# A hybrid decoder layer: attention merges moved from ScalarE and GpSimd to VectorE, branch sums to VectorE, x rows loaded ahead of merged blocks

## The chip, the cores and the metric

The kernel runs on one NeuronCore of a Trainium2 chip. The time is the device time of one execution in microseconds; the median of several runs is compared. TensorE (PE, with its weight loads PEld), VectorE (DVE), ScalarE (ACT) and GpSimd (POOL) each work through a queue of their own in order. SyncE (SP) issues nearly all DMA transfers, also in order: an issue that waits holds back those behind it. PSUM holds the matmuls' results; a tile of it is free again once another engine has read it.

## What is computed

One decoder layer over 2048 tokens with 1024 channels, in float32:

```
h = rms_norm(x); proj = h @ w_in                      # 1024 x 9224
A: gated DeltaNet   q,k,v = silu(conv(proj)); chunk inverse; scan over time with states S
                    y_dn  = (rms_norm(o_dn) * silu(z)) @ w_branch_dn
B: dilated window attention, three groups (window, dilation), each with output o_g and log denominator
                    alpha = softmax over the groups' log denominators
                    o_swa = sum_g alpha_g * o_g
                    y_swa = (o_swa * silu(z)) @ w_branch_swa
merged = sigmoid(g_dn) * y_dn + sigmoid(g_swa) * y_swa
x      = x + merged @ w_out
```

The change touches three places: the sum over groups in `o_swa` (called a merge here), the sum of the two gated branches in `merged`, and the loads of the rows of `x` that the last line adds.

## The kernel before, in words

Each float32 operand is split into a high and a low part, so that a product is three matmuls. The program has these stages.

- Up to about 970 us: normalisation and the attention columns of `w_in`, with the attention itself beside them. For each of 16 tiles of 128 tokens it leaves in DRAM (`oscr`) the three groups' unnormalised outputs, four heads of 128 channels, each with two more columns: the negated score maximum and the sum of exponentials.
- Up to about 2003 us: 24 column blocks of 128 (z columns, DeltaNet columns, then 16 gate blocks), `cunits`, L710. A block is four units of 512 tokens, 24 matmuls of 128x512 each (L723 to L725). A gate unit's result stands in one of three PSUM buffers `mm` until ScalarE has taken its tanh (`g_block`, L1159) into one of two `gt` buffers, which SyncE stores to `gscr` (L1160). Beside these units run first the DeltaNet blocks' own work, then the chunk inverse on VectorE, the scan (16 steps over time, L1031 to L1146), and the merges.
- Branch products, about 2003 to 2207 us (`fin_y`): 8 blocks `nb` of 256 tokens, 8 pieces `m` of 128 output channels, each piece 24 matmuls of 128x256 (L1345 to L1347). L1349 gates both branches in PSUM on VectorE, L1351 adds them, L1352 stores the sum to `mscr`. `o_plan` and `o_prep` beside it load, transpose (L1314) and gate (L1315, with z from L1307) the next block's inputs. `g_load` (L1333) loads the gates three pieces ahead. Four times `wo_chunk` prepares a quarter of `w_out`.
- Output projection from 2207 us (`group`): 8 groups of 256 tokens, seven products of 12 matmuls of 128x512 each (L1424) in a Strassen-like scheme. `m_load` (L1359) loads the merged blocks, `m_op` splits them (L90, L91) and forms their sums (L1380); x rows (`xo`, L1398) are added to the products on GpSimd (L1408) and VectorE (L1411).

What orders the work: a counter `tick` goes up at every `hook()`, which stands after every six matmuls of a column unit and every twelve of a branch piece, and `self.at(d, f)` emits `f` at d ticks from now. In the branch products this is the order of all queues. In the column blocks from the inverse on, and in the output projection, a scheduler may still reorder what was so emitted.

A merge (`combine(t)`, L1255) before: VectorE takes the minimum of the negated maxima (L1252), GpSimd the differences (L1263), ScalarE their exponential (L1266), GpSimd the shares (L1267 to L1271; the reciprocal is a power of -1). ScalarE scales the 12 outputs of 128x128 (L1275), GpSimd adds the groups in two instructions of 128x512 (L1279), SyncE stores the result to `osd` (L1281). The input tile `oc` has two buffers: the load of merge t+2 (L1247) waits for the store of merge t. Merges are numbered 0 to 15 here. 6 to 15 run after the scan, beside the gate units.

In the scan, L1065 and L1072 prepare the block that a step multiplies with; L1084 and L1086 are products with the states, L1088 makes `rr` from them on VectorE, L1091 `qs` on ScalarE, L1095 multiplies `rr`, L1097 takes `vn`, L1101 and L1106 use it, L1103 updates the states on VectorE, L1122 scales the result, L1124 stores it.

Of the kernel before, what the change touches and what calls it, by code (L numbers as in the profile page):

```python
# [6 lines left out]
F32 = mybir.dt.float32  # L7
F32R = mybir.dt.float32r
AF = mybir.ActivationFunctionType
ALU = mybir.AluOpType  # L10
PSUM = bass.MemoryType.PSUM

P = 128
# [4 lines left out]
H = 4  # L18
# [25 lines left out]
def dr(ap, off, dims):  # L44
    return bass.AP(tensor=ap.tensor, offset=ap.offset + off, ap=[list(d) for d in dims])


class Net:
# [1184 lines left out]

    def comb_setup(self, M):
        self.M, self.ocs = M, {}
        self.mone = self.cb.tile([P, 4], F32, name="mone", bufs=1)
        self.nc.gpsimd.memset(self.mone, -1.0)
        self.comb_load(0)
        self.comb_load(1)
        self.at(6, lambda: self.comb_min(0))  # L1240
        self.at(11, lambda: self.combine(0))

    def comb_load(self, t):
        oc = self.ocs[t] = self.cb.tile([P, G, H, 130], F32, name="oc", bufs=2)
# [2 lines left out]
        self.nc.sync.dma_start(oc.rearrange("p g h c -> p (g h c)"),  # L1247
                               dr(self.oscr, t * P * G * H * 130, [[G * H * 130, P], [1, G * H * 130]]))

    def comb_min(self, t):  # L1250
        self.cs = self.cb.tile([P, 4, 12], F32, name="cs", bufs=2)
        self.nc.vector.tensor_reduce(out=self.cs[:, 0, 0:4].unsqueeze(2), in_=self.ocs[t][:, :, :, 128].rearrange("p g h -> p h g"),  # L1252
                                     axis=mybir.AxisListType.X, op=ALU.min)

    def combine(self, t):  # L1255
        nc, cb, V = self.nc, self.cb, self.nc.gpsimd
        oc, sm = self.ocs.pop(t), self.cs
        if 0 < t < 15:
            self.comb_load(t + 1)
        nm, ls = oc[:, :, :, 128], oc[:, :, :, 129]  # L1260
        mn, e, c, r = sm[:, 0, 0:4], sm[:, 1, :].rearrange("p (g h) -> p g h", h=H), \
            sm[:, 2, :].rearrange("p (g h) -> p g h", h=H), sm[:, 3, 0:4]
        V.tensor_tensor(out=e, in0=mn.unsqueeze(1).to_broadcast([P, G, H]), in1=nm, op=ALU.subtract)  # L1263

        def share():
            nc.scalar.activation(e, e, AF.Exp)  # L1266
            V.tensor_tensor(out=c, in0=e, in1=ls, op=ALU.mult)  # L1267
            V.tensor_tensor(out=r, in0=c[:, 0], in1=c[:, 1], op=ALU.add)
            V.tensor_tensor(out=r, in0=r, in1=c[:, 2], op=ALU.add)
            V.tensor_tensor(out=r, in0=r, in1=self.mone, op=ALU.pow)  # L1270
            V.tensor_tensor(out=c, in0=e, in1=r.unsqueeze(1).to_broadcast([P, G, H]), op=ALU.mult)  # L1271

        def weigh(g):
            for h in range(H):
                nc.scalar.activation(oc[:, g, h, 0:P], oc[:, g, h, 0:P], AF.Identity, scale=c[:, g, h:h + 1])  # L1275

        def add(g):
            o = oc[:, 0, :, 0:P]
            V.tensor_tensor(out=o, in0=o, in1=oc[:, g, :, 0:P], op=ALU.add)  # L1279
            if g == 2:  # L1280
                nc.sync.dma_start(dr(self.osd, t * P * 512, [[512, P], [P, H], [1, P]]), o)  # L1281
        self.at(2, share)
        for g in range(G):
            self.at(5 + g, lambda g=g: weigh(g))
        for g in (1, 2):
            self.at(6 + g, lambda g=g: add(g))
        if t < 15:
            self.at(9, lambda: self.comb_min(t + 1))
            self.at(15, lambda: self.combine(t + 1))

    def o_load(self, t):
        nc, fp = self.nc, self.fp
# [28 lines left out]
    def o_plan(self, nb, d):  # L1321
        self.z = getattr(self, "z", {})
        for j, (t, b) in enumerate(((2 * nb, 0), (2 * nb, 1), (2 * nb + 1, 0), (2 * nb + 1, 1))):
            self.at(max(1, d + 3 * j - 8), lambda t=t, b=b: self.z_load(t, b))
            self.at(d + 3 * j, lambda t=t, b=b: self.o_prep(t, b))
            if b and nb < 7:
                self.at(d + 3 * j + 1, lambda t=t: self.o_load(t + 2))
# [7 lines left out]
    def fin_y(self, nb, m):  # L1335
        nc = self.nc
        self.g_load(8 * nb + m + 3)
        gt = self.gt.pop(8 * nb + m)
        pr = self.ps.tile([P, 512], F32, name="mm", bufs=3)
        for b in range(2):  # L1340
            o = pr[:, b * 256:(b + 1) * 256]
            oh, ol = self.o_tiles(nb, b)
            for k in range(4):
# [4 lines left out]
            self.hook()  # L1348
        nc.vector.scalar_tensor_tensor(out=gt, in0=gt, scalar=1.0, in1=pr.rearrange("p (b c) -> p b c", c=256),  # L1349
                                       op0=ALU.add, op1=ALU.mult)  # L1350
        nc.gpsimd.tensor_tensor(out=gt[:, 0, :], in0=gt[:, 0, :], in1=gt[:, 1, :], op=ALU.add)  # L1351
        self.at(2, lambda: nc.sync.dma_start(dr(self.mscr, nb * P * 2048 + m * 256, [[2048, P], [1, 256]]), gt[:, 0, :]))  # L1352

    def m_load(self, g):
        if g < 8:
# [36 lines left out]
    def group(self, g):  # L1392
        nc, V, p2 = self.nc, self.nc.vector, self.p2
        acc, hold, xo = {}, {}, {}

        def x_load(t, c):
            xo[t, c] = p2.tile([P, 512], F32, name="xo", bufs=4)
            nc.sync.dma_start(xo[t, c], dr(self.i["x"], (2 * g + t) * P * D + c * 512, [[D, P], [1, 512]]))  # L1398
# [13 lines left out]
            nc.sync.dma_start(dr(self.out, (2 * g + t) * P * D + c * 512, [[D, P], [1, 512]]), add)  # L1412
        for t, c in ((0, 0), (0, 1), (1, 1), (1, 0)):
            x_load(t, c)
        for i, (_, tgt, first, wn) in enumerate(PROD):
            q = 7 * g + i
            self.at(1, lambda q=q: self.m_op(q + 4))
# [30 lines left out]
    def run(self):  # L1448
# [55 lines left out]
        sm = pool(cst, "sm")  # L1504
# [78 lines left out]
            self.flush()  # L1583
        fst.close()
        self.p2 = pool(p2st, "p2", "right")
        self.m_load(1)
        for g in range(8):
            self.group(g)
        self.flush()
# [43 lines left out]
```

## Time and profile before

| what | value |
|---|---|
| median of 3 runs | 2374.9 us (2374.2 to 2382.52) |
| the profiled execution | 2375.45 us, of it 2373.6 us span |
| granted TensorE clock, mean | 0.989 |
| busy: TensorE, VectorE, ScalarE, GpSimd | 2282.9, 1353.3, 979.7, 1004.8 us |
| TensorE idle, 1660 to 1866 us (scan) | 13.8 us |
| 1866 to 2003 us (gate units, merges 6 to 15) | 15.0 us |
| 2003 to 2207.5 us (branch products) | 7.3 us |
| 2207.5 to 2244 us (first output group) | 5.8 us |
| from 2244 us | 3.8 us |

Rows of the profile name an engine, a line of the kernel, the operation, and what it writes and reads. In a row of a timeline the start and the duration in us stand first; in a grouped row the count, the total in us and the mean in ns follow. A bracket with an arrow tells how long the engine had stood idle before the instruction and what ended that wait. SPq is SyncE's queue of DMA issues. A mean granted clock below 1 says that for part of the time TensorE ran slower.

### The profile page before, as it was taken

Reading aid. Unit: us, or ns where it says so; the run is one execution under the profiler, and the core shown is the slowest. Engines: PE = TensorE matmul, PEld = TensorE weight load, DVE = VectorE, ACT = ScalarE, POOL = GpSimd, SP = SyncE. Lnnn points to the kernel's source line nnn. Section 1 sums busy time; section 2 is a strip of 40 time slices with the busy share of each in tenths; the row PEclk is TensorE's granted clock in tenths of the full one; section 3 lists DMA queues with packets and bytes.
Section 4 is the critical chain, followed back from the end, with each engine's and each line's share of the span. In section 5 each row is a group of like instructions: output and inputs, shape, how many; then the busy total and the mean of one; then the engine's idle time right before and its main releaser. Section 6 shows DMA issues by size and latency. Waiting matters only on the chain. (4 is left out here: it accounts for less than half of the span.)

```text
span 2373.6 us, 43873 instructions
## 1 busy us (share of the span) xinstructions
PE 2282.9 (96%) x15120; PEld 2069.9 (87%) x15120; DVE 1353.3 (57%) x2788; ACT 979.7 (41%) x3151; POOL 1004.8 (42%) x1460
## 2 busy tenths in 40 slices
PE   7999999989999999999999999999999989999999
PEld 7999999889999999787788788888788767999787
DVE  6566586693545545536777759998244202544553
ACT  5345466642434435445666641111444454211221
POOL 6374275574303203304667441121433453554543
PEclk9999999999999999999999999999999999999999
DMA  9989989858887888744544452224677765788742
GB/s 304 322 280 312 286 276 281 263 168 260 254 262 241 257 262 274 240 122 105 147 115 114 119 143 65 78 71 147 191 200 207 220 205 173 229 263 239 245 153 92
DMA packets 557270, 485.82 MB, mean 205 GB/s; under 512 B 68280, under 2 KB 517112, under 8 KB 554104
## 3 DMA queue, kind: packets, MB, share of 16 engines
q1 hardware_dynamic: 556760, 482.95, 66.4%
q8 instruction: 120, 1.97, 0.3%
q14 instruction: 102, 0.84, 0.1%
q10 hardware_dynamic: 288, 0.07, 0.0%
HBM read 280.23 MB, written 202.67 MB: 203 GB/s over the span
## 5 line engine op out<-in xcount | busy, mean ns | idle before, releaser
L723 PE MATMUL mm<-hh,w 128*128 128x512 f32 x1152 | 464.8, 403 | 13.7 <-ACT gt L1159 13.7
L725 PE MATMUL mm<-hh,w 128*128 128x512 f32 x1152 | 458.9, 398 | 0.0
L724 PE MATMUL mm<-hl,w 128*128 128x512 f32 x1152 | 458.0, 398 | 0.0
L436 PE MATMUL mm<-w,hh 128*128 128x256 f32 x1760 | 326.8, 285 | 0.0
L723 PEld LDWEIGHTS mm<-hh,w 128*128 128x128 f32 x1152 | 220.7, 192 | 62.0 <-ACT gt L1159 16.7
L436 PEld LDWEIGHTS mm<-w,hh 128*128 128x128 f32 x1760 | 269.9, 189 | 0.0
L725 PEld LDWEIGHTS mm<-hh,w 128*128 128x128 f32 x1152 | 217.7, 189 | 47.3
L436 PE MATMUL mm<-hh 128*128 128x256 f32 x880 | 256.4, 291 | 0.0
L724 PEld LDWEIGHTS mm<-hl,w 128*128 128x128 f32 x1152 | 218.3, 190 | 42.5
L91 POOL TENSOR_TENSOR w<-raw,w 128x512 fp32r<-128x512 f32 x68 | 99.2, 1461 | 361.8 <-ACT w L90 361.6
L436 PE MATMUL mm<-hl,hh 128*128 128x256 f32 x880 | 248.8, 283 | 0.9 <-POOL hl L298 0.9
L436 PE MATMUL mm<-hh,hl 128*128 128x256 f32 x880 | 248.7, 283 | 0.0
L436 PE MATMUL mm<-w,hl 128*128 128x256 f32 x880 | 247.6, 281 | 0.0
L610 DVE CUSTOM_DVE_ANT_0 p<-sc,mask 128x128 f32<-128x128 f32 (+1 forms) x192 | 70.0, 365 | 214.9 <-PE sc L607 83.3
L371 POOL TENSOR_SCALAR st<-st 128x4 f32<-128x4 f32 x96 | 20.5, 213 | 370.1 <-ACT junk L370 368.1
L436 PEld LDWEIGHTS mm<-hl,hh 128*128 128x128 f32 x880 | 168.2, 191 | 1.3 <-POOL hl L298 1.3
L436 PEld LDWEIGHTS mm<-hh 128*128 128x128 f32 x880 | 168.2, 191 | 0.0
L436 PEld LDWEIGHTS mm<-hh,hl 128*128 128x128 f32 x880 | 168.0, 191 | 0.0
L436 PEld LDWEIGHTS mm<-w,hl 128*128 128x128 f32 x880 | 165.3, 188 | 0.0
L837 DVE SCALAR_TENSOR_TENSOR acc<-xr,cw,acc 128x512 f32<-128x512 f32 x144 | 121.2, 841 | 16.7 <-ACT acc L835 11.5
L594 ACT ACTIVATE kq<-tp 128x256 fp32r<-128x256 f32 x148 | 56.5, 382 | 178.6 <-PE tp L587 177.6
L370 ACT ACTIVATE junk<-rec 128x128 f32<-128x128 f32 x288 | 89.4, 310 | 54.9 <-DVE rec L364 47.3
(353 smaller groups left out, 5815.2 us busy)
## 6 DMA issues: line engine op xcount, KB each, us to landing
wdr<-w SPq DMA_DIRECT2D x56, 512.0 KB, 4.5
w<-wdr SPq DMA_DIRECT2D x54, 512.0 KB, 5.0
qk<-qks SPq DMA_DIRECT2D x212, 128.0 KB, 3.9
qks<-rec SPq DMA_DIRECT2D x96, 256.0 KB, 3.0
raw<-in_w_in_dram SPq DMA_DIRECT2D x68, 256.0 KB, 3.3
gscr<-gt SPq DMA_DIRECT2D x64, 256.0 KB, 2.8
gt<-gscr SPq DMA_DIRECT2D x64, 256.0 KB, 5.3
wdr<-hh SPq DMA_DIRECT2D x28, 512.0 KB, 4.8
```

The lines of the kernel that those rows point to most:

```text
L91: eng.tensor_tensor(out=l, in0=raw, in1=h.bitcast(F32), op=ALU.subtract)
L370: nc.scalar.activation(self.junk, src[:, j * P:(j + 1) * P], AF.Square, accum_out=st[:, j:j + 1])
L371: nc.gpsimd.tensor_scalar(out=st[:, 0:4], in0=st[:, 0:4], scalar1=1.0 / P, scalar2=EPS, op0=ALU.mult, op1=ALU.add)
L436: mm = lambda x, y, **kw: nc.tensor.matmul(o, x, y, skip_group_check=True, **kw)
L594: nc.scalar.activation(h, src, AF.Copy)
L610: nc.vector.tensor_tensor_reduce(out=p[:, lo:hi], in0=sc[:, lo:hi], in1=self.mask[:, slot * P + lo:slot * P + hi], scalar=3e38, scale=-SCA ...
L723: nc.tensor.matmul(pr, wh[:, k, :], a, start=(k == 0), stop=False)
L724: nc.tensor.matmul(pr, wh[:, k, :], b, start=False, stop=False)
L725: nc.tensor.matmul(pr, wl[:, k, :], a, start=False, stop=(k == KT - 1))
L837: nc.vector.scalar_tensor_tensor(out=acc, in0=xr[:, j:j + 512], scalar=w[:, j:j + 1], in1=acc, op0=ALU.mult, op1=ALU.add)
```

## The change

A merge is made by VectorE, but for the exponential on ScalarE and the two group sums, which stay on GpSimd: minimum, differences, products, sum, reciprocal, shares, and three weighings of 128x512 (one per group, the shares broadcast along the channels) in place of ScalarE's 12. `combine` starts at tick 8 and then every 13 ticks (before 11 and 15) and takes the minimum itself; the exponential is emitted with it. The two gated branches are added by VectorE; their store is emitted one tick after the piece (before two). `z_load` is emitted 6 ticks before its use (before 8), though never before the block's first tick. The load of merged block 1 comes after the first group's four loads of x rows.

```diff
 def comb_setup(self, M):
     self.M, self.ocs = M, {}
-    self.mone = self.cb.tile([P, 4], F32, name="mone", bufs=1)
-    self.nc.gpsimd.memset(self.mone, -1.0)
     self.comb_load(0)
     self.comb_load(1)
-    self.at(6, lambda: self.comb_min(0))
-    self.at(11, lambda: self.combine(0))
+    self.at(8, lambda: self.combine(0))
...
-def comb_min(self, t):
-    self.cs = self.cb.tile([P, 4, 12], F32, name="cs", bufs=2)
-    self.nc.vector.tensor_reduce(out=self.cs[:, 0, 0:4].unsqueeze(2), in_=self.ocs[t][:, :, :, 128].rearrange("p g h -> p h g"),
-                                 axis=mybir.AxisListType.X, op=ALU.min)
...
 def combine(self, t):
-    nc, cb, V = self.nc, self.cb, self.nc.gpsimd
-    oc, sm = self.ocs.pop(t), self.cs
+    nc, cb, V = self.nc, self.cb, self.nc.vector
+    oc = self.ocs.pop(t)
     if 0 < t < 15:
         self.comb_load(t + 1)
+    sm = cb.tile([P, 4, 12], F32, name="cs", bufs=2)
...
+    V.tensor_reduce(out=mn.unsqueeze(2), in_=nm.rearrange("p g h -> p h g"), axis=mybir.AxisListType.X, op=ALU.min)
     V.tensor_tensor(out=e, in0=mn.unsqueeze(1).to_broadcast([P, G, H]), in1=nm, op=ALU.subtract)
+    nc.scalar.activation(e, e, AF.Exp)
     def share():
-        nc.scalar.activation(e, e, AF.Exp)
         V.tensor_tensor(out=c, in0=e, in1=ls, op=ALU.mult)
-        V.tensor_tensor(out=r, in0=c[:, 0], in1=c[:, 1], op=ALU.add)
-        V.tensor_tensor(out=r, in0=r, in1=c[:, 2], op=ALU.add)
-        V.tensor_tensor(out=r, in0=r, in1=self.mone, op=ALU.pow)
+        V.tensor_reduce(out=r.unsqueeze(2), in_=c.rearrange("p g h -> p h g"), axis=mybir.AxisListType.X, op=ALU.add)
+        V.reciprocal(r, r)
         V.tensor_tensor(out=c, in0=e, in1=r.unsqueeze(1).to_broadcast([P, G, H]), op=ALU.mult)
     def weigh(g):
-        for h in range(H):
-            nc.scalar.activation(oc[:, g, h, 0:P], oc[:, g, h, 0:P], AF.Identity, scale=c[:, g, h:h + 1])
+        V.tensor_tensor(out=oc[:, g, :, 0:P], in0=oc[:, g, :, 0:P], in1=c[:, g, :].unsqueeze(2).to_broadcast([P, H, P]),
+                        op=ALU.mult)
     def add(g):
         o = oc[:, 0, :, 0:P]
-        V.tensor_tensor(out=o, in0=o, in1=oc[:, g, :, 0:P], op=ALU.add)
+        nc.gpsimd.tensor_tensor(out=o, in0=o, in1=oc[:, g, :, 0:P], op=ALU.add)
...
     for g in range(G):
-        self.at(5 + g, lambda g=g: weigh(g))
+        self.at(3 + g, lambda g=g: weigh(g))
     for g in (1, 2):
-        self.at(6 + g, lambda g=g: add(g))
+        self.at(5 + g, lambda g=g: add(g))
     if t < 15:
-        self.at(9, lambda: self.comb_min(t + 1))
-        self.at(15, lambda: self.combine(t + 1))
+        self.at(13, lambda: self.combine(t + 1))
...
 # o_plan
-        self.at(max(1, d + 3 * j - 8), lambda t=t, b=b: self.z_load(t, b))
+        self.at(max(1, d + 3 * j - 6), lambda t=t, b=b: self.z_load(t, b))
...
 # fin_y
-    nc.gpsimd.tensor_tensor(out=gt[:, 0, :], in0=gt[:, 0, :], in1=gt[:, 1, :], op=ALU.add)
-    self.at(2, lambda: nc.sync.dma_start(dr(self.mscr, nb * P * 2048 + m * 256, [[2048, P], [1, 256]]), gt[:, 0, :]))
+    nc.vector.tensor_tensor(out=gt[:, 0, :], in0=gt[:, 0, :], in1=gt[:, 1, :], op=ALU.add)
+    self.at(1, lambda: nc.sync.dma_start(dr(self.mscr, nb * P * 2048 + m * 256, [[2048, P], [1, 256]]), gt[:, 0, :]))
...
 # group, after the four x_load calls
+    if g == 0:
+        self.m_load(1)
...
 # run
-    self.m_load(1)
     for g in range(8):
         self.group(g)
```

Since a scheduler orders the merges among the other work, three places show where the instructions now stand. First ScalarE's queue beside the gate units, after the scan; before (L1266 exponential, L1275 scaling, L1159 gate, L90 a weight split):

```order
L1266 ACTIVATE cs<-cs 128x12
L90 ACTIVATE w_228<-raw 128x512
L1275 ACTIVATE oc<-oc,cs 128x128 x8
L90 ACTIVATE w_228<-raw 128x512
L1159 ACTIVATE gt<-mm 128x512
L1275 ACTIVATE oc<-oc,cs 128x128 x4
L1266 ACTIVATE cs<-cs 128x12
```

and now, where the exponential is L1258:

```order
L1258 ACTIVATE cs<-cs 128x12
L1159 ACTIVATE gt<-mm 128x512
L1258 ACTIVATE cs<-cs 128x12
L90 ACTIVATE w_228<-raw 128x512 x2
L1159 ACTIVATE gt<-mm 128x512
L1258 ACTIVATE cs<-cs 128x12
L1159 ACTIVATE gt<-mm 128x512
```

The scalings are gone from between the gates; one exponential per merge still stands there. Second, VectorE's queue at the scan's start, before:

```order
L1252 TENSOR_REDUCE cs<-oc 128x4 x2
L1065 TENSOR_TENSOR zs<-sc,nbr 64x256
L1088 SCALAR_TENSOR_TENSOR rr<-sc,ksn,rec 128x128 x4
```

and now (the same seven rows stand twice, for merges 0 and 1, ahead of L1065):

```order
L1256 TENSOR_REDUCE cs<-oc 128x4
L1257 TENSOR_TENSOR cs<-cs,oc 128x12
L1261 TENSOR_TENSOR cs<-cs,oc 128x12
L1262 TENSOR_REDUCE cs<-cs 128x4
L1263 RECIPROCAL cs<-cs 128x4
L1264 TENSOR_TENSOR cs<-cs 128x12
L1267 TENSOR_TENSOR oc<-oc,cs 128x4x128 x3
L1065 TENSOR_TENSOR zs<-sc,nbr 64x256
L1088 SCALAR_TENSOR_TENSOR rr<-sc,ksn,rec 128x128 x4
```

Two whole merges now precede the scan's first instruction on VectorE; merges 2 to 5 stand between `rr` of later steps in the same way. Third, SyncE's queue at the first output group, before:

```order
L1352 DMA mscr<-gt_25984 128x256
L1359 DMA o<-mscr 128x1024
L1359 DMA mt<-mscr 128x1024 x2
L1398 DMA xo<-in_x_dram 128x512 x4
L1412 DMA out_dram<-xo 128x512
```

and now:

```order
L1344 DMA mscr<-gt_25822 128x256
L1351 DMA o<-mscr 128x1024
L1390 DMA xo<-in_x_dram 128x512 x4
L1351 DMA mt<-mscr 128x1024 x2
L1404 DMA out_dram<-xo 128x512
```

The x rows stand ahead of merged block 1 (`mt`) and still behind the last store of the branch products. With it VectorE's first L1405 and L1411 and GpSimd's three L1408 of that group moved ahead of the work on block 1.

## Prediction

> **What bounds the kernel now.** I read the page first, then busy time by stretch, then TensorE's waits in each stretch, then single rows. The stretches are: the scan (from 1660 us), the gate units beside the last merges (1866), the branch products (2003), the first group of the output projection (2207.5) and the rest.
>
> ```profile
> span 2373.6 us, 43873 instructions
> PE 2282.9 (96%) x15120; PEld 2069.9 (87%) x15120; DVE 1353.3 (57%) x2788; ACT 979.7 (41%) x3151; POOL 1004.8 (42%) x1460
> ...
> 1660.00:1866.00 206.00, 192.22 (x1279) 166.25 (x1278) 74.63 (x241) 86.81 (x327) 79.05 (x211) 0.98 0.71 204
> 1866.00:2003.00 137.00, 122.02 (x510) 97.04 (x509) 15.57 (x33) 67.70 (x194) 71.69 (x107) 0.96 0.66 204
> 2003.00:2207.50 204.50, 197.19 (x1649) 196.25 (x1648) 97.38 (x130) 37.96 (x64) 110.09 (x107) 0.98 0.81 242
> 2207.50:2244.00 36.50, 30.74 (x124) 23.97 (x124) 23.44 (x26) 10.00 (x17) 18.31 (x13) 0.95 0.66 209
> 2244.00:2373.60 129.60, 125.83 (x549) 102.78 (x548) 55.52 (x73) 24.55 (x40) 51.73 (x41) 1.00 0.40 130
> ```
>
> After the stretch and its length stand the busy times of PE, PEld, DVE, ACT and POOL, then the granted clock. TensorE is the bound everywhere, so only its gaps can be won: 13.8, 15.0, 7.3, 5.8 and 3.8 us of idle time. Its work does not change. Who ends the gaps, with total, times and longest:
>
> ```profile
> PE sc L1084 <- ACT vb L1072: 3.5, 1, 3.5
> PE tp L1095 <- DVE rr L1088: 2.9, 3, 1.2
> PE sc L1062 <- ACT qs L1091: 2.1, 1, 2.1
> PE po L1101 <- ACT vn L1097: 1.6, 1, 1.6
> ...
> PE mm L723 <- ACT gt L1159: 13.7, 7, 4.1
> ...
> PE mm L1345 <- DVE gt L1349: 7.1, 4, 4.3
> ...
> PE mm L1424 <- DVE hold L1411: 3.3, 1, 3.3
> PE mm L1424 <- DVE hold L1405: 2.5, 2, 1.4
> ```
>
> The largest is ScalarE's gate activation, which frees the PSUM buffer of a gate unit. A gap also costs something behind it:
>
> ```profile
> 1911.13 0.40 PE L724 MATMUL mm<-hl,w 128*128 128x512 f32 x1
> 1911.36 0.40 PE L725 MATMUL mm<-hh,w 128*128 128x512 f32 x1
> 1915.86 0.79 PE L723 MATMUL mm<-hh,w 128*128 128x512 f32 x1 [4.10 <-ACT gt L1159]
> 1916.45 0.63 PE L724 MATMUL mm<-hl,w 128*128 128x512 f32 x1
> 1916.88 0.63 PE L725 MATMUL mm<-hh,w 128*128 128x512 f32 x1
> ...
> 1918.59 0.56 PE L723 MATMUL mm<-hh,w 128*128 128x512 f32 x1
> ```
>
> Starts stand 0.23 us apart before the gap and 0.43 after it, from 1915.86 to 1918.59: six intervals took 2.7 us instead of 1.4, some 1.4 lost again. At 0.23 us the 510 matmuls from 1866 to 2003 need 117 us, so that stretch loses 20 us, 15 of them idle; by the same count (124 matmuls, 28.5 us) the first group loses 8.
>
> **Part 1, the last ten merges (beside the gate units).** What sets their pace:
>
> ```profile
> 1953.37 0.32 SPq L1247 DMA_DIRECT2D oc<-oscr  x1
> ...
> 1957.76 0.17 DVE L1252 TENSOR_REDUCE cs<-oc 128x4 f32<-128x12 f32 x1 [8.92 <-DMA oc<-oscr]
> ...
> 1957.98 0.52 SPq L1281 DMA_DIRECT2D osd<-oc  x1
> ...
> 1960.64 0.32 SPq L1247 DMA_DIRECT2D oc<-oscr  x1
> ...
> L1275 ACT ACTIVATE oc<-oc,cs 128x128 f32<-128x128 f32 x127 | 39.4, 389 | 22.7 <-POOL cs L1271 20.4 <-DMA osd<-oc 2.3
> ...
> L1279 POOL TENSOR_TENSOR oc<-oc 128x512 f32<-128x512 f32 x22 | 28.4, 1291 | 18.6 <-ACT oc L1275 18.1
> ...
> 1873.90:1968.20 94.30, 6.92 (x12) 0.96 0.67 212
> ...
> 1873.90:1968.30 94.40, 1.98 (x10) 0.96 0.67 212
> ```
>
> The last two rows are gate activations and merge exponentials on ScalarE: ten merges, nine intervals, take 94.3 us, with 12 gate units between them. Twelve units of 24 matmuls at 0.23 need 66 us. So it is the merges that hold the gates up, and with them TensorE, which has three PSUM buffers to run ahead in. They stand in one ScalarE queue: 12 scalings of 0.39 us behind shares that GpSimd makes, and gates behind them. In the change ScalarE keeps one exponential of 0.21 us per merge, and VectorE, busy for 15.6 of 137 us here, takes the rest. The nearest rows for its instructions:
>
> ```profile
> L1380 DVE TENSOR_TENSOR raw<-mt x8: 675/692/1778, 2219.3 to 2319.4; 128x512 f32<-128x512 f32 x8
> ...
> L1109 DVE TENSOR_TENSOR qs<-tp,qs x32: 416/421/425, 1684.4 to 1865.4; 128x256 f32<-128x256 f32 x32
> ...
> L1351 POOL TENSOR_TENSOR gt<-gt x64: 727/742/1195, 2006.5 to 2209.7; 128x256 f32<-128x256 f32 x64
> ```
>
> A 128x512 weighing is 0.69 us, or 1.78 where it meets GpSimd; the small ones are 0.17 as in L1252. One merge in the change: load to minimum 4.4 (1953.37 to 1957.76), six small instructions 1.0, exponential and hand-overs 0.4, first weighing 0.7, then two GpSimd sums 2.6 (which cover the other two weighings), and from the store's issue to the next load 2.7 (1957.98 to 1960.64), with 1.0 for the issue and queueing: 12.8 us. Two buffers alternate, so 6.4 per merge; with every weighing at 1.78 and the sums slowed alike, some 15.6, or 7.8. Nine intervals are 58 to 70 us, against TensorE's 66. The gates would no longer wait, or by little, and the exponential that still stands between two gates finds its input there. I take 17 of the 20 us. Bounds: 5 (pace stays near 9 us, from loads behind SyncE's queue) and 20.
>
> The Trainium skill, "GPSIMD Engine Reference", section 8 "Key points", speaks against this: GpSimd shares its SBUF interfaces with VectorE, and VectorE instructions with two SBUF inputs contend. The trace agrees with the 1.78 us row. By that rule alone all 30 weighings here would be slow, and the term would be its 7.8 us pace, some 3 us worse than mine.
>
> **Part 2, the scan's first step.** Before, merges 0 and 1 hold ScalarE while the scan's first block waits:
>
> ```profile
> 1663.63 0.18 DVE L1252 TENSOR_REDUCE cs<-oc 128x4 f32<-128x12 f32 x1 [1.84 <-DMA oc<-oscr]
> ...
> 1673.62 0.43 DVE L1065 TENSOR_TENSOR zs<-sc,nbr 64x256 f32<-64x256 f32 x1 [9.81 <-PE sc L1062]
> ...
> 1675.48 3.61 ACT L1275 ACTIVATE oc<-oc,cs 128x128 f32<-128x128 f32 x12 [3.62 <-POOL cs L1271]
> ...
> 1679.00 0.36 ACT L1072 ACTIVATE vb<-sc 64x256 f32<-64x256 f32 x1
> ```
>
> In the change VectorE does both merges ahead of L1065. Merge 1's load is there at 1663.6; a merge is 1.0 + 0.4 + 3 x 0.69 = 3.5 us, so both are done by about 1669, four before L1065 is due. L1072 then runs at about 1675: 4.1 us sooner, and 1.4 of slow clock. **-5.5**, bounds 0 and -7.
>
> **Part 3, the other merges in the scan (2 to 5).** ScalarE's qs and vn waits, 2.1 and 1.6, go. New: mul, sum, reciprocal, share and a first weighing, 4 x 0.17 + 0.69 = 1.4 us, stand ahead of rr on VectorE. Six filler matmuls (1.4 us) lie between those products and L1095; merge 2 has 60. What slips through I put at 1.7 in all: **-2**, bounds -6 and, where every merge stands in the open, the price of the third rival.
>
> **Part 4, branch products.** 64 sums go from GpSimd (0.74, up to 1.2) to VectorE, at most 0.42 each by L1109: 27 us on an engine with 97.4 of 204.5 busy. It is still not the bound. Stores leave a step sooner and may wait for VectorE, with gate loads behind them. One row shows what stops TensorE:
>
> ```profile
> 2166.75 0.75 DVE L1315 SCALAR_TENSOR_TENSOR z<-tp,dnw,z 128x512 f32<-128x512 f32 x1 [7.22 <-DMA z<-zscr]
> ```
>
> VectorE waits for z, the PSUM releases queue behind it. In the change the first two z loads of a block keep their tick; the third and fourth go two ticks later and no longer share the DMA with them, nor hold SyncE for a z buffer. I take 3 of the 7.1 us. Bounds -9 (all, with slow clock) and +10 (each of the four w_out chunks meets a fuller VectorE, 2.5 each).
>
> **Part 5, first group.**
>
> ```profile
> 2212.24 2.63 SPq L1398 DMA_DIRECT2D xo<-in_x_dram  x4
> ...
> 2220.56 0.69 DVE L1411 TENSOR_TENSOR xo<-mm,xo 128x512 f32<-128x512 f32 x1 [0.54 <-DMA xo<-in_x_dram]
> ```
>
> x rows land behind 1 MB of merged block 1; GpSimd adds them only then, and TensorE stands still 5.8 us. Moved ahead, they leave 1 us sooner, and 1 MB, 5 us at the stretch's 209 GB/s, no longer lies before them; transfers overlap, so I take 3 us sooner. VectorE and GpSimd now take them first. Block 1 in turn lands up to 5 us later. It was there before 2220.6, since VectorE had used it ahead of L1411, so by 2225.6 at the latest; its first product is due after seven products of twelve matmuls, at 2207.5 + 7 x 2.75 = 2226.8. That is cover, if thin. **-5.5** of 8, bounds 0 and -8.
>
> **Sum**, against the profiled 2375.45: -17 - 5.5 - 2 - 3 - 5.5 = -33, so 2342.4; that execution lies 0.5 us above the runs' median, so **2342 us**.
>
> **The rivals.** (1) Loads set the merges' pace: SyncE issues stores, gate stores and loads in one order, and the pace stays near 9 us. Part 1 gives 5: 2354. For it: the row at 1957.76, where VectorE waits 8.92 us for a load; against it: each load waits for the store of the merge two before it, which ends sooner in the change. (2) Handed back in the branch products: VectorE's sums hold up its PSUM releases, and SyncE, waiting for a sum, holds the gate loads behind the store. Part 4 then costs 10 instead of winning 3, and part 5 wins nothing because the last store is late: 2342 + 13 + 5.5 = about 2361. For it: the 7.22 us row, behind which releases queue already; against it: GpSimd's sum took 0.74 to 1.2 us and came after the same release, so a store's input is ready sooner, not later. (3) Slower: VectorE becomes the scan's bound. Its queue is in order, and a minimum that waits for its load holds rr and the state update behind it.
>
> ```profile
> L1252 DVE TENSOR_REDUCE cs<-oc 128x4 f32<-128x12 f32 x6 | 1.0, 174 | 20.5 <-DMA oc<-oscr 20.5
> ```
>
> Six merges in the scan waited 20.5 us for loads, 3.4 each. If that wait, a fully contended merge of 0.8 + 3 x 1.78 = 6.1 us and 1.4 of slow clock lie open at merges 2 to 5, they cost 44, parts 2 and 3 win nothing, and with 25.5 from the other parts it ends at 2393. From 6.4 us open per merge on it is slower than before. Against it: the third load now goes ahead of the stores of the scan's first results, which had held it back. (4) It does little: ScalarE's waits return as waits for VectorE's weighings one for one, and only part 5 is left, 2370.
>
> **Chances.** Forecast 0.54, (1) 0.16, (2) 0.14, (3) 0.09, (4) 0.07. A measurement of this kernel tells about 0.5% from no change: faster is below 2363, slower above 2386.8. Forecast, (1) and half of (2), whose time lies at the edge, are faster, 0.77; the other half and (4) the same, 0.14; (3) slower, 0.09. The sum of the lower bounds is 2323 and of the nearer upper ones about 2360, but they will not all fall on one side: from 2326 up to 2368 the range takes in (1) and (2) and leaves out (3), (4) and small tails, 2 in 10.
>
> **What would show it.** Right: no L723 wait on the gate activation above 1 us; merges 6 to 15 in 58 to 75 us; L1072's first run near 1675; x rows landed by 2217 of the old clock. Wrong: L1095 or L1084 waiting for VectorE's rr in many steps; gates still waiting; new L1345 waits on VectorE's sums.

## The result and the profile after

The changed kernel takes 2359.83 us (median of 4 runs, 2356.9 to 2362.6) against 2376.61 for the kernel before beside it: a ratio of 0.9926, 95% interval 0.9901 to 0.9950. Run once more on another occasion the ratio was 0.9908 (0.9889 to 0.9927). It is faster by some 17 to 21 us; the prediction was 2342, a gain of 33. One execution in the second set of the changed kernel, and one of the kernel with the x rows alone (below), took some 9410 us; these two are in the medians but not in the ratios.

To see where the other half went, the program is cut at points that both kernels have: the first and the last L1062 (the scan), the first matmul of the branch products, their last one, and the end. The page's first lines of the changed kernel, and busy time by stretch between these points (columns as in the prediction), first of the change:

```profile
span 2360.8 us, 43608 instructions
PE 2280.7 (97%) x15120; PEld 2069.1 (88%) x15120; DVE 1438.4 (61%) x2980; ACT 923.6 (39%) x2959; POOL 930.5 (39%) x1299
...
1678.30:1857.30 179.00, 169.30 (x1160) 145.74 (x1160) 79.69 (x259) 64.16 (x251) 61.97 (x163) 0.99 0.71 202
1857.30:1993.50 136.20, 128.61 (x571) 104.99 (x572) 53.15 (x124) 33.02 (x73) 53.43 (x48) 0.95 0.70 215
1993.50:2196.80 203.30, 195.92 (x1646) 194.52 (x1645) 127.64 (x193) 37.88 (x64) 63.35 (x44) 0.99 0.81 244
2196.80:2360.80 164.00, 157.08 (x677) 127.27 (x676) 80.19 (x99) 34.76 (x57) 70.23 (x52) 0.99 0.47 150
```

and of the kernel before:

```profile
1672.90:1854.80 181.90, 168.12 (x1144) 146.14 (x1143) 69.03 (x221) 75.98 (x289) 66.00 (x179) 0.97 0.68 195
1854.80:2002.70 147.90, 132.92 (x587) 106.62 (x587) 20.82 (x51) 73.95 (x215) 76.42 (x122) 0.97 0.66 205
2002.70:2207.00 204.30, 196.99 (x1647) 196.01 (x1646) 97.38 (x130) 37.98 (x64) 110.09 (x107) 0.98 0.81 242
2207.00:2373.60 166.60, 157.07 (x677) 127.24 (x675) 78.95 (x98) 34.55 (x57) 70.04 (x53) 0.99 0.46 148
```

The four stages became shorter by 2.9, 11.7, 1.0 and 2.6 us, 18.2 in all. The two profiled executions differ by 12.8, because the changed one came to the scan 5.4 us late (1678.3 instead of 1672.9). That part of the program is untouched. In the fourteen profiles of this study, none of whose edits touches it, the scan began between 1669.9 and 1682.6 us; so these 5.4 us are chance, and stage lengths tell more than spans.

Who ends TensorE's waits in the change, stage by stage. In this kernel L1258 is the exponential, L1267 a weighing, L1272 a sum, L1274 the store of a merge, L1244 its load; L1306 and L1307 are the transposes and z products (L1314 and L1315 before), L1341 the gating (L1349), L1395 to L1403 the uses of the output products (L1403 to L1411), L1418 their matmuls (L1424).

```profile
PE sc L1062 <- DMA t<-tscr: 4.7, 4, 2.5
PE tp L1095 <- DVE rr L1088: 3.1, 4, 1.0
...
PE tp L1306 <- DMA o<-odn: 4.9, 1, 4.9
PE mm L723 <- ACT gt L1159: 2.7, 1, 2.7
...
PE mm L1337 <- DVE gt L1341: 5.6, 4, 2.9
...
PE mm L1418 <- ACT hold L1395: 2.3, 1, 2.3
```

The waits that the prediction wanted gone are nearly gone: the gate activations' 13.7 us are 2.7, and the scan's waits for ScalarE (3.5, 2.1, 1.6) don't appear. But others stand in their place: the scan waits 4.7 us for t (before 1.4), the gate stage 4.9 for o (before 1.3), the second output group 2.3 for a copy on ScalarE. Together they are 9.2 us longer than before, the largest of what the prediction left out, and the experiments go after them.

### The profile page after: what moved, and what is told of

It reads as the page before. It is cut to its first block, busy times and chain, and to the rows that moved or that the text cites. A ratio compares the mean times of both kernels' runs of the same rounds, so it can differ in the third digit from the quotient of the medians.

```text
span 2360.8 us, 43608 instructions
## 1 busy us (share of the span) xinstructions
PE 2280.7 (97%) x15120; PEld 2069.1 (88%) x15120; DVE 1438.4 (61%) x2980; ACT 923.6 (39%) x2959; POOL 930.5 (39%) x1299
## 5 line engine op out<-in xcount | busy, mean ns | idle before, releaser
L91 POOL TENSOR_TENSOR w<-raw,w 128x512 fp32r<-128x512 f32 x68 | 99.1, 1461 | 371.2 <-ACT w L90 371.1
L613 ACT ACTIVATE p<-p,ol 128x128 f32<-128x128 f32 (+1 forms) x192 | 88.1, 459 | 61.6 <-DVE ol L610 61.4
```

The lines of the kernel that those rows point to most:

```text
L91: eng.tensor_tensor(out=l, in0=raw, in1=h.bitcast(F32), op=ALU.subtract)
L613: self.at(1, lambda: nc.scalar.activation(p[:, lo:hi], p[:, lo:hi], AF.Exp, bias=ol[:, 128:129], scale=-1.0, accum_out=ol[:, 129:130]))
```

## The experiments

All times are medians; each ratio is against the kernel before, run beside it. "Scan and gates" runs from the first L1062 to the first matmul of the branch products (one column, because the scheduler moves some column-unit matmuls over the border between the two).

| kernel | time, us | ratio (95%) | scan and gates | branch | output |
|---|---|---|---|---|---|
| before (its profile) | 2376.6 | 1 | 329.8 | 204.3 | 166.6 |
| the change | 2359.8 | 0.9926 (0.9901 to 0.9950) | 315.2 | 203.4 | 163.9 |
| the change again | 2358.8 | 0.9908 (0.9889 to 0.9927) | 313.8 | 201.2 | 164.1 |
| merges alone | 2364.8 | 0.9938 (0.9923 to 0.9952) | 315.2 | 203.3 | 166.3 |
| branch sums alone | 2378.8 | 0.9997 (0.9982 to 1.0011) | 336.8 | 201.7 | 166.4 |
| x rows alone | 2377.2 | 0.9987 (0.9970 to 1.0004) | 331.0 | 204.1 | 164.1 |
| change, z earlier | 2357.1 | 0.9900 (0.9882 to 0.9918) | 314.7 | 202.7 | 164.1 |
| change, transposes later | 2352.2 | 0.9890 (0.9865 to 0.9915) | 306.5 | 203.8 | 163.9 |
| change, three merge buffers | 2428.6 | 1.0213 (1.0197 to 1.0228) | 308.8 | 261.5 | 179.7 |
| change, stores by GpSimd | 2357.2 | 0.9919 (0.9898 to 0.9940) | 316.4 | 203.5 | 164.1 |
| change, block 1 between x rows | 2355.4 | 0.9919 (0.9894 to 0.9944) | 313.0 | 201.3 | 167.6 |
| transposes later, block 1 split by VectorE | 2353.7 | 0.9894 (0.9876 to 0.9913) | 305.2 | 203.0 | 164.8 |
| the same, blocks 1 and 2 | 2349.2 | 0.9869 (0.9848 to 0.9890) | 314.9 | 201.7 | 159.8 |
| the same, all blocks from 1 on | 2351.2 | 0.9882 (0.9862 to 0.9901) | 304.8 | 202.7 | 159.9 |

### The change once more

> The change itself once more, beside the run above, to see how far stages and time vary: scan and gate stage together 315 us in the change's profile, branch products 203.4, output 163.9; everything ahead of the scan, which no edit touches, took 1678.3 us in it and 1672.9 before. If that difference of 5.4 us is chance, it comes out elsewhere between 1669 and 1683 here, and the other stages within 2 us.

Measured: the scan begins at 1676.1 us, scan and gates take 313.8, the branch products 201.2, the output 164.1. So the start varies by some 10 us, as expected, and the stages come back within 1.4 us but for the branch products, which are 2.2 off. One profile is not always that good: the kernel with the branch sums alone has the code of the kernel before ahead of its branch products, and its scan and gates took 336.8 us against 329.8. The time is 20.9 us below the kernel before beside it.

### The parts of the change, one by one

Each part was put alone into the kernel before, as the diff of the change has it (merges: `comb_setup` and `combine`; branch sums: `fin_y` and `z_load`; x rows: the move of `m_load(1)`).

> The kernel before with the merges' edit alone. Theory A (each edit brings in its own stage what the two profiles show there, and nothing elsewhere): the scan, from its first L1062 to its last, 181.9 before, is 179.0; from there to the first matmul of the branch products, 147.9 before, is 136.2; the branch products and the output projection stay as before at 204.3 and 166.6; in all 2376.6 - 14.6 = 2362. Theory B (the forecast's 24.5 is there, and the later edits or the scheduler's other order ate part of it): 2352, with the gate stage near 129. Merges' exponentials 6 to 15: 84 us as in the change by A (loads set the pace), under 75 by B.

> The kernel before with the branch sums on VectorE, their store a tick sooner, and z loaded two ticks later. Theory A: the branch products, 204.3 before and 203.4 in the change, shorten by about 1; time 2376. The forecast's term: -3, 2373.6. Rival (the later z load gives back what the sooner stores win): the wait of VectorE for z stays near 25 us in all, as in both profiles (26.3 and 25.4), and TensorE still waits some 7 us for L1349.

> The kernel before with the x rows of the first output group loaded ahead of merged block 1. Theory A: the output projection, 166.6 before, becomes 163.9 as in the change, because a new wait of some 2.3 us in the second group (products waiting for ScalarE's copy L1403 behind its splits of block 1) takes half of what the x rows win; time 2374. The forecast's term alone: -5.5, so 161.1 and 2371.

Measured: -0.62%, -0.03% and -0.13%, that is 14.8, 0.7 and 3.1 us. Their sum of 18.6 is what the whole change brings, so the parts don't eat each other's gain, as far as intervals of some 3.5 us either way for each can tell: Theory A holds, and Theory B, by which the merges alone reach 2352, falls (2364.8, interval at best 2361). The gate stage with the merges alone waits as in the change:

```profile
PE tp L1306 <- DMA o<-odn: 4.8, 1, 4.8
PE mm L723 <- ACT gt L1159: 3.0, 1, 3.0
```

The x rows alone give 164.1 us of output stage, not the forecast's 161. The branch sums alone shorten their stage by 2.6 us (201.7), close to the forecast's 3, but in the other profiles that have them it takes 201.2 to 203.8, with the old sums 203.3 to 204.3: a gain of 1 to 2 us that no time here tells from nothing.

### z loaded earlier again

```diff
-        self.at(max(1, d + 3 * j - 6), lambda t=t, b=b: self.z_load(t, b))
+        self.at(max(1, d + 3 * j - 8), lambda t=t, b=b: self.z_load(t, b))
```

> The change with the z loads at 8 ticks before their use again, all else as in the change. If the later z load gave back what the sooner stores won, the branch products take 201 us or less instead of 203.4, VectorE waits for z under 15 us in all instead of 25.4, and the time is 2357. If z is held up by its three buffers or by SyncE's waits for the sums (58 us in the change), nothing changes: 203 to 204, 2360; a longer stage (205 and more) says that SyncE held behind z loads costs more than it brings.

Measured: branch products 202.7 us, inside what the change itself shows; the wait for z is the same:

```profile
DVE z L1307 <- DMA z<-zscr: 25.4, 6, 7.9
...
DVE z L1307 <- DMA z<-zscr: 25.7, 6, 7.7
```

The first row is the change, the second this kernel. The tick of the z load doesn't matter. So the reason that the prediction gave for a gain here (two z loads later, off the DMA of the other two) isn't one; what remains of the gain comes from the sums or from their earlier store, which no run separates.

### The transposes' wait for o

How the 4.9 us arise in the change, from the timelines of GpSimd, SyncE and TensorE:

```profile
1873.36 3.04 POOL L1272 TENSOR_TENSOR oc<-oc 128x512 f32<-128x512 f32 x2 [2.06 <-DVE oc L1267]
...
1876.42 0.56 SPq L1274 DMA_DIRECT2D osd<-oc  x1
...
1878.36 0.39 SPq L1289 DMA_DIRECT2D o<-odn  x1
...
1882.27 1.09 PE L1306 MATMUL tp<-ident,o 128*128 128x128 f32 x4 [4.88 <-DMA o<-odn]
```

SyncE stood from 1871 to 1876.4 before the store of a merge, until GpSimd had ended its sums; behind it stood the load of o, and behind that the transposes. Before, the same transposes ran 24.7 us after the scan's last L1062 (1879.53), now 25.0: this chain didn't become faster, TensorE only reached it sooner. The edit lets the first block's transposes and z loads come three ticks later:

```diff
-            self.o_plan(0, 8)
+            self.o_plan(0, 11)
```

> The change with the first block's transposes (L1306) and z loads emitted three ticks later; on TensorE the first transposes then stand 18 matmuls (4.1 us) later. In the change TensorE waits 4.9 us there for the load of o (before: 1.3), since SyncE stands behind the store of a merge whose sums GpSimd ends at 1876.4. Theory C (this wait is the largest piece of what the forecast of the gate stage missed, and costs its 4.9 us and about 1.4 of slow clock): the wait falls below 1 us and the gate stage, 136 us in the change, takes 130 to 132; time 2355. Rival (the saved time runs into the next late thing, as it did here): the stage stays above 134, with longer waits for the gate activation or for z.

Measured: scan and gates 306.5 us, 8.7 less than in the change. The ratio of 0.9890 overlaps the change's, so it is the stage that shows the gain, and it does so again: from the last L1062 to the branch products the four profiles with this edit (three of them in kernels further down) take 126 to 129 us, and five without it (the change, twice, the merges alone, z earlier, block 1 between x rows) 134 to 137.

```profile
1858.10:1985.60 127.50, 124.67 (x567) 101.87 (x566) 53.60 (x124) 32.86 (x73) 53.57 (x48) 0.99 0.75 230
...
PE mm L723 <- ACT gt L1159: 2.2, 1, 2.2
PE tp L1306 <- DMA o<-odn: 0.7, 1, 0.7
```

Theory C holds, with more than its price: the wait is 4.2 us shorter, and the granted clock of the stage is 0.99 instead of 0.95. Counting by how much the starts of the column-unit matmuls are more than 0.23 us apart (less 0.4 us for the transposes themselves), the change loses 5.4 us in this gap and 2.1 of slow clock behind it, 2.9 and 2.9 at the gate wait; here it is 0.9 and 0.1, 2.3 and 1.7. Not all of that is the edit's doing: the change once more had a gate wait of 3.05 us with no slow clock behind it.

### Three buffers for the merges' input

```diff
-        oc = self.ocs[t] = self.cb.tile([P, G, H, 130], F32, name="oc", bufs=2)
+        oc = self.ocs[t] = self.cb.tile([P, G, H, 130], F32, name="oc", bufs=3)
...
-        if 0 < t < 15:
-            self.comb_load(t + 1)
+        if t < 14:
+            self.comb_load(t + 2)
```

For the room, `gt4` has 5 instead of 7 and `z` 2 instead of 3 buffers, which makes the branch products 261.5 us; only what lies ahead of them is compared.

> The change with three input buffers for the merges, loaded two merges ahead (room for it is made by 5 instead of 7 gate buffers and 2 instead of 3 z buffers in the branch products, so that stage isn't compared). The merges 6 to 15 take 84 us in the change, where VectorE waits 2.7 to 7.7 us for a load in each. If two buffers set that pace (each load waits for a store, lands 4.7 to 7.7 us later): 70 us or less, VectorE's waits for loads under 15 us in all instead of 45, and the remaining gate wait of 2.7 us gone; gate stage 132 to 133. If SyncE's order and the scheduler set it, 80 us or more and the gate wait stays.

Measured: scan and gates 308.8 us, 6.4 less than in the change. The remaining gate wait is gone; VectorE's waits for merge loads in the gate stage, first of the change and then of this kernel, are shorter (in all 33.4 instead of 45.1 us, not under 15):

```profile
DVE cs L1256 <- DMA oc<-oscr: 28.2, 7, 7.7
...
DVE cs L1256 <- DMA oc<-oscr: 19.3, 7, 7.0
```

But the merges don't run at a faster pace: the exponentials of merges 8 to 15 stand between 1874.61 and 1936.61 us, seven intervals of 8.9, against 1891.19 to 1951.62, or 8.6, in the change. They end 15 us sooner since one merge more was done in the scan and the next began at once. So a third buffer alone doesn't quicken the pace, and the 70 us are not met. Whether the gate wait went through the third buffer or through the merge that moved into the scan isn't separated, nor is what sets the pace: SyncE's order, the loads' landing or the order that the scheduler chose.

### Stores of the merges by GpSimd

```diff
-                nc.sync.dma_start(dr(self.osd, t * P * 512, [[512, P], [P, H], [1, P]]), o)
+                nc.gpsimd.dma_start(dr(self.osd, t * P * 512, [[512, P], [P, H], [1, P]]), o)
```

> The change with the merges' stores issued by GpSimd itself, behind its sums, instead of SyncE. If SyncE's waiting for those sums is what makes o late in the gate stage and the t loads late in the scan, both waits shrink: transposes' wait 4.9 to under 2, L1062's waits for t 4.7 to under 2 in all, gate stage 130 to 132, scan 175 to 177; time 2350. If the issue on GpSimd costs it a microsecond or more each, its chain to the state outputs (L1116 to L1120) is late and the scan gets longer than 179. Its scan has another order of instructions, so a difference of 2 us there proves nothing.

Measured: no gain, 316.4 us; the scan is 5.9 us shorter and the gate stage 7.1 longer. The two waits do shrink, as the expectation's first case says, though not below 2 in the scan:

```profile
PE sc L1062 <- DMA t<-tscr: 3.4, 2, 2.0
...
PE mm L723 <- ACT gt L1159: 7.5, 4, 5.0
PE tp L1306 <- DMA o<-odn: 1.8, 1, 1.8
```

The transposes' wait falls from 4.9 to 1.8: the store that waited in SyncE's queue was most of its cause. What was won there returned as gate waits of 7.5 us, where the exponential of a merge stands in ScalarE's queue without its input and a gate behind it. The scheduler set another order here, so why the merges' inputs came later isn't shown.

### Block 1 and the x rows

In the change the x rows land in time, and the waits move. The timelines of SyncE, VectorE and ScalarE:

```profile
2199.79 2.32 SPq L1390 DMA_DIRECT2D xo<-in_x_dram  x4
...
2206.17 0.69 DVE L1403 TENSOR_TENSOR xo<-mm,xo 128x512 f32<-128x512 f32 x1 [2.41 <-DMA xo<-in_x_dram]
...
2211.15 1.78 DVE L1372 TENSOR_TENSOR raw<-mt 128x512 f32<-128x512 f32 x1
...
2224.93 0.58 ACT L1395 ACTIVATE hold<-mm 128x512 f32<-128x512 f32 x1
```

L1403 has its x row 9.3 us after the stage began at 2196.9, where before it had it after 13.6 (2220.56 against 2207.0). But VectorE then works almost without a pause from 2210.1 to 2229.5, several of its sums at 1.6 to 1.78 us, each of which began while a GpSimd instruction ran; ScalarE waits for these sums with its splits, and behind them stands L1395, which frees a PSUM tile. First, block 1's load was put between the x rows:

```diff
         for t, c in ((0, 0), (0, 1), (1, 1), (1, 0)):
             x_load(t, c)
-        if g == 0:
-            self.m_load(1)
+            if g == 0 and (t, c) == (0, 1):
+                self.m_load(1)
```

> The change with merged block 1's loads between the second and the third x row: they are issued about 1.2 us sooner, and TensorE's order is the same. If block 1, late behind the x rows, makes the new wait of 2.3 us in the second group, it falls to 1 or less and the output stage, 163.9 us, takes 161.5 to 162.5. If VectorE and GpSimd are simply full there (VectorE is busy without a pause from 2209.9 to 2229.5, many of its sums at 1.78 instead of 0.68 us beside GpSimd), nothing changes, 163.5 to 164.5.

Measured: 167.6 us, worse. The work on block 1 begins sooner and now stands ahead of the products' L1397 and L1403 in VectorE's queue; TensorE waits 2.3 and 3.1 us for them. The wait for L1395 did fall, from 2.3 to 0.4 us, so block 1 was late for it; but an earlier load only moves the wait, because VectorE's long sums come earlier with it. Then GpSimd's splits of block 1 were given to VectorE (here with the later transposes, which touch another stage):

```diff
-        self.split(part[name] if name in part else ss[name], *self.m_slot(q), V if name in part else nc.gpsimd)
+        self.split(part[name] if name in part else ss[name], *self.m_slot(q), V if name in part or g == 1 else nc.gpsimd)
```

> The change with the transposes three ticks later (as in the run before), and all low-part splits (L91) of merged block 1 on VectorE instead of three of them on GpSimd; TensorE's order is the same as there. Theory D (in the first output groups VectorE is held up by sharing its way to memory with GpSimd: sums of 0.68 us take 1.78): without GpSimd's splits in that stretch the sums stay near 0.7, which frees some 8 us of VectorE and pays for three more splits of 0.7; the wait for L1395 (2.3 us) and L1403 (0.7) go, the output stage, 163.9, takes 160 to 162; time 2350. Rival (VectorE is short of time in any case and the splits only make its queue longer): the output stage takes 164 to 168, time 2352 to 2356.

Measured: 164.8 us, no gain, as the rival has it; but its timeline shows the reason at work:

```profile
2208.43 0.69 DVE L1372 TENSOR_TENSOR raw<-mt,raw 128x512 f32<-128x512 f32 x1
...
2212.35 2.13 POOL L91 TENSOR_TENSOR hl<-raw,hh 128x512 fp32r<-128x512 f32 x1 [9.87 <-ACT hh L90]
...
2217.89 1.74 DVE L1372 TENSOR_TENSOR raw<-mt 128x512 f32<-128x512 f32 x1
2219.55 0.68 DVE L1397 TENSOR_TENSOR hold<-mm,hold 128x512 f32<-128x512 f32 x1
...
2220.29 0.79 PE L1418 MATMUL mm<-hh 128*128 128x512 f32 x1 [3.52 <-DVE hold L1397]
```

While GpSimd has nothing to split, the sums take 0.69 us; from its first split of block 2 on most take 1.74 to 1.77, and L1397, which frees a PSUM tile, stands behind three of them. The wait had moved on by one block. So block 2 was added, and in a second kernel all later blocks:

```diff
-V if name in part or g == 1 else nc.gpsimd)
+V if name in part or g in (1, 2) else nc.gpsimd)
```

> As the run with block 1's low-part splits on VectorE, and block 2's too. There the sums took 0.69 us until GpSimd began block 2's splits at 2212.4, then 1.77 again, and the first products of the second group waited 3.5 us for L1397 behind three such instructions. Theory D, mended (VectorE is slowed by GpSimd's splits, whichever block's, until the two first groups' work is done): the wait of 3.5 falls under 1 us, output stage 160.5 to 162.5 instead of 164.8 (163.9 in the change), time 2349 to 2351. Rival (VectorE's queue is simply too full): 164 or more.

> As that, with the low-part splits of all blocks from 1 on on VectorE, so that GpSimd keeps only the additions of x rows. By theory D the first two groups are as in the run above, and the later ones have no long sums either: output stage 160 to 162.5. By the rival VectorE (80 of 164 us busy in the change, some 28 splits of 0.7 more) holds up products in the later groups: 165 or more.

Measured: output stage 159.8 and 159.9 us, 4.1 below the change, even under the range that I had given. Of the first kernel:

```profile
2191.90:2351.70 159.80, 155.22 (x677) 126.02 (x675) 78.33 (x107) 34.43 (x57) 57.46 (x44) 1.00 0.48 154
...
PE mm L1418 <- DVE hold L1403: 0.7, 1, 0.7
```

VectorE does more instructions (107 instead of 99) in less busy time (78.3 instead of 80.2 us). In the stretch of the two first groups eleven of twelve sums (L1372) now take 0.67 to 0.69 us. Theory D holds; the rival, a VectorE that is simply too full, falls. A split is also shorter on VectorE (mostly 0.68 us, on GpSimd 1.29 to 1.76); what that adds to the gain isn't separated. With ratios of 0.9869 and 0.9882 these two are also the fastest of the study; the change has 0.9926 and 0.9908, with intervals that just touch theirs, and both also hold the later transposes (0.9890 alone), so it is the stage that shows the difference. The first one's scan took 186.1 us at a granted clock of 0.95 in its profile, where the same code took 177.6 to 180.3 in eight others, so a comparison of spans would hide the gain.

## Why the prediction was right or wrong

**Right:** the sign, the range (2326 to 2368), and that the parts add. The sum was nearly twice too large: -33, where the stages show -18.2 and the times -17 to -21. The range held the result because it was drawn to take in rivals (1) and (2), not because the terms were right; its lower bounds add up to 50 us and so to 2325, not the 2323 given, on which nothing else hangs. Of its four signs of being right two came (L1072; x rows landed at 2216.3 of the old clock) and two did not (a gate wait of 2.7 us was left; the merges took 84 us).

**Part 1 (-17, measured about -9).** The gate stage is 11.7 us shorter, but 12 of its column-unit matmuls, 2.8 us, now lie in the scan (510 and 498 in the single rows). That the gates would stop waiting came true (13.7 to 2.7 us). Two steps failed. The first: I called the merges' pace the cause and gave 58 to 70 us for nine intervals. The pace hardly changed:

```profile
1867.70:1951.70 84.00, 1.98 (x10) 0.92 0.74 233
...
1934.29 0.21 ACT L1258 ACTIVATE cs<-cs 128x12 f32<-128x12 f32 x1 [7.53 <-DVE cs L1257]
1934.41 0.59 ACT L1159 ACTIVATE gt<-mm 128x512 f32<-128x512 f32 x1
...
1944.98 0.17 DVE L1256 TENSOR_REDUCE cs<-oc 128x4 f32<-128x12 f32 x1 [7.66 <-DMA oc<-oscr]
...
1945.46 0.21 ACT L1258 ACTIVATE cs<-cs 128x12 f32<-128x12 f32 x1 [10.46 <-DVE cs L1257]
1945.58 1.08 ACT L1159 ACTIVATE gt<-mm 128x512 f32<-128x512 f32 x2
```

Nine intervals take 84 us, 9.3 each. The load, which I had at 4.4 us from one row, took 4.6 to 11.0, 6.0 in the median (6.1 already before: one row was too few), and the two sums 3.05 instead of 2.6. So rival (1) had the pace right ("near 9 us") and the price wrong: it gave 5 us, measured are 9. The forecast's reason was wrong too. It said that an exponential between two gates would find its input there. In eight of the ten merges it doesn't: ScalarE stands idle for 3 to 10 us until VectorE has the differences, and in five of these a gate starts 0.12 us behind the exponential, as in the rows. What changed is how late the gates are. From the end of a unit's last matmul to the start of its gate it was 2.8 to 17.8 us beside the merges before, over 11 us (two units, as far as three PSUM buffers let TensorE run ahead) in eight of twelve units. In the change it is 0.1 to 2.0 us until 1899, then up to 13.2, over 11 only once, and that once is the gate wait of 2.7 us. The likely reason is that the 4.7 us of scalings per merge are gone from that queue; it was not tested apart from the pace. The second failed step is an omission: I didn't ask what TensorE would reach next. The transposes wait for o at 24.7 us after the scan, whatever the merges do; that took back some 6 us (7.5 in gap and slow clock, 1.5 before), and the later transposes gave 8.7 back.

**Parts 2 and 3 (-5.5 and -2, measured about -5.7 together).** The scan is 2.9 us shorter with 2.8 us more work in it. L1072 runs 2.0 us after the first L1062 instead of 6.1: the 4.1 us that part 2 gives, to the tenth. The cover was thinner than foreseen, though: VectorE was done with merge 1 only 2.2 us ahead of L1065, not 4, since three of the small instructions took 1.1 to 1.3 us instead of 0.18. With the slow clock that part 2 counts, next to nothing is left for part 3. ScalarE's two waits (3.7 us) went as foreseen, but TensorE waits 3.3 us more for t, which the part left out. The load of t stands in SyncE's queue behind a store that waits for VectorE, as in the longest case:

```profile
1777.88 2.52 POOL L91 TENSOR_TENSOR w<-raw,w 128x512 fp32r<-128x512 f32 x2
1777.96 2.52 DVE L1122 TENSOR_SCALAR os<-qs,oss 128x128 f32<-128x128 f32 x2 [1.03 <-POOL oss L1120]
...
1776.95 3.90 SPq L1124 DMA_DIRECT2D odn<-os  x2
...
1782.16 1.56 SPq L1050 DMA_DIRECT2D t<-tscr  x1
...
1787.80 0.41 PE L1062 MATMUL sc<-t,lo 64*64 64x64 f32 x4 [2.50 <-DMA t<-tscr]
```

Here no merge is in the way. The two L1122 take 1.28 and 1.32 us, where 61 of the 64 take 0.28 or 0.29, and the first two rows show what ran beside them: two splits on GpSimd (L91), each from just before the start of one L1122 to just before its end. That is some 2 us of the 2.5, as an estimate from these durations. The kernel before has five such L1122, so the change didn't bring them.

Rival (3) named VectorE's queue as the danger in the scan; the waits for rr are as before (3.1 and 2.9), so it fell.

**Part 4 (-3, measured -1 to -3).** The 64 sums cost VectorE 30 us (97.4 to 127.6), near the 27 foreseen, and hurt nobody. The z loads, on which the term rested, made no difference. Rival (2) fell: but for the kernel with fewer z and gate buffers, the stage takes 201.2 to 203.8 us with the new sums, 203.3 to 204.3 with the old.

**Part 5 (-5.5, measured -2.6).** The x rows came 4.3 us sooner, more than the 3 assumed. The step that failed is the cover for block 1: I counted whether it lands before its first product (it does) and not what its work costs VectorE when it is squeezed into the same 20 us as GpSimd's splits. The prediction had the very row, a sum of 1.78 instead of 0.69 us, and used it for the merges' weighings, where it never happened (0.682 to 0.695 us in all 48). It happened here. By the Trainium skill's "SBUF — State Buffer", section "Who interferes with whom", a VectorE instruction with two SBUF inputs contends with a GpSimd instruction that reads SBUF, and the contention is an exclusive lock. The trace agrees in this stage: L1372 has two inputs in SBUF and takes up to 1.78 us, L1397 with one input in PSUM takes 0.68 in the same stretch. In the merges it was some of the small instructions that met GpSimd (least, median and longest time in ns):

```profile
L1261 DVE TENSOR_TENSOR cs<-cs,oc x16: 172/182/1279, 1667.9 to 1951.9; 128x12 f32<-128x12 f32 x16
```

For the weighings GpSimd's side paid. The first of a merge's two sums starts while the third weighing runs and takes 1.65 to 1.68 us; the second takes 1.27 to 1.31.

**Rival (4)** (only part 5 is left, 2370) fell with the merges alone, which bring 14.8 us without part 5.

## What to carry to other kernels

Before a wait is counted as won, follow TensorE to the next thing that it needs: a chain through a store and a load does not speed up with the engine in front of it, and here moving its consumer by three ticks was worth 8.7 us in one line. When an engine's instructions are moved, ask in which stretches VectorE's instructions with two SBUF inputs will meet GpSimd's, and count those sums at the long duration; giving such work to one engine made the stage 4.1 us shorter here. And compare stages between fixed points rather than spans, since code that no edit touched varied by 12 us here, and take more than one profile, since a scan of the same code once took 186 us instead of 178 to 180.

## What was not expected of the hardware

The price of a gap jumps, and it isn't fixed. In the gate stages of all fourteen profiles, the matmuls ran at full speed again at once behind every wait for a gate activation of up to 1.9 us. Of the nineteen longer ones, 2.04 to 4.98 us, sixteen cost another 1.4 to 2.9 us through a slower clock, which in some of them set in later than the gap; three, of 2.05, 2.12 and 3.05 us, cost nothing more. In the kernel before after a wait of 2.06 us, and in the change once more after one of 3.05:

```profile
1938.10 0.50 PE L723 MATMUL mm<-hh,w 128*128 128x512 f32 x1 [2.06 <-ACT gt L1159]
...
1945.41 0.50 PE L723 MATMUL mm<-hh,w 128*128 128x512 f32 x1 [3.05 <-ACT gt L1159]
...
1938.10:1941.10 3.00, 3.00 (x10) 0.72 0.91 345
...
1945.40:1948.40 3.00, 2.99 (x13) 1.00 0.75 198
```

The last two rows are the 3 us behind each: a granted clock of 0.72 and of 1.00. What decides between the two isn't shown. The prediction had one price, 1.4 us, for any gap; it should have asked first which gaps are longer than 2 us, and taken the price for those as likely, not certain.
